# Samples' state increments as four 32-partition tiles, and other changes of order, in a one-core hybrid decoder layer

## The chip, the cores and the metric

The kernel runs on one core of a Trainium2 chip. Its time is device microseconds of one execution; the median of 3 runs of the kernel before is 1911.06 us (1909.26 to 1911.51). PE is the matrix engine (TensorE), DVE the vector engine, ACT the scalar engine, POOL GpSimd, SP the engine that issues the DMAs.

## What is computed

One layer is applied to a prompt (1 sequence of 1024 tokens) and to a group of samples (8 sequences of 8 new tokens, with caches and states). Both go through the same weights, so the kernel lays the 64 sample tokens behind the 1024 prompt tokens: 1088 columns. The layer projects to q, k, v, to a gate, to the state-space inputs z, x, B, C, dt and to two merge gates; it runs dilated window attention in three groups and a Mamba-2 scan (SSD), projects both branches, merges them and projects once more:

```python
# per state-space head group; b sequences, c chunks, l and s tokens, n = 128 states, p = 64
cb = jnp.einsum('bclgn,bcsgn->bcgls', cm, bm)
y_diag = jnp.einsum('bcgls,bgecls,bcsgep->bclgep', cb, decay, xdt)
decay_to_end = jnp.exp(da_cs[..., -1:] - da_cs)
states = jnp.einsum('bclgn,bgecl,bclgep->bcgepn', bm, decay_to_end, xdt)
def step(carry, inp):
    tot, st = inp
    return jnp.exp(tot)[..., None, None] * carry + st, carry
final, prev = lax.scan(step, init, ...)
y_off = jnp.einsum('bclgn,bcgepn,bgecl->bclgep', cm, prev, jnp.exp(da_cs))
...
merged = jax.nn.sigmoid(g_a) * a_out + jax.nn.sigmoid(g_b) * m_out
return x + gate[:, None, :] * (merged @ w_out)
```

For the samples a chunk is one sequence of 8 tokens. `states` of a sample is then a product over those 8 tokens only: its 128 states by the 128 channels of two heads. The sum of the decayed old state and this increment is an output for each sample and head.

## The kernel before

**Tiles.** Channels lie on the partitions, the 1088 tokens along the row, cut into chunks of 368, 368 and 352 columns for projections. A projection of 128 output channels takes 8 input tiles x 3 chunks x 3 matmuls (`mm3`, L195 to L200): weights and activations are split in a high and a low fp32r half, and high*high, low*high and high*low are summed in a PSUM bank named `pj`. The other matmuls have fp32 operands and go through `mm` (L206) or, as transposes, through `turn` (L210); both lines stand for many places, so the names of the tiles tell the places apart.

**Order.** On PE the order is the order of the Python calls, as long as `region` (L481 to L1105) is open. The projections run in a fixed list (`run`, L260). Between them a small planner, `Order` (L58), slips in the side work, which is written as generators: each `yield ns,` in such a generator asks that so many planned nanoseconds of projections pass before the next piece; `yield key, ns` counts them from the end of a named projection. The planner's nanoseconds are constants of the code. DVE, ACT, POOL and SP are ordered by a scheduler.

**Stages.** After norms and early projections (to about 65 us) comes attention with the projections of q, k, v (to 768 us), the state-space stage with the projections of B, C, x and z (to about 1545 us), the two branch projections and the output projection `fo` (to 1902.5 us).

**Attention** (`prompt_group`, L590). For each head pair and group, `scores(i)` makes scores s with two row tiles of 64 partitions (one per head) and the exponentials pr on DVE and ACT; `turned(i)` transposes pr through the bank pt to pT; `values(i)` makes o with column tiles of 64. The loop at its end calls `values(i - 2)`, `turned(i - 1)` and `scores(i)`.

**State space** (`side`, L924, and `x_tile`, L962). There are four groups. Each makes B and C (`conv_job`, L844), turns B's tokens onto the partitions (`to_tokens`, bank tt, result Bk), and makes C's products with B (bank cb). Then come four tiles of x, two heads each. A tile loads the decay table `csb` by DMA from `cs_d` (L965) and prepares it on DVE (L969, L972), ACT and DVE; turns its tokens (tt, result xdt); makes the prompt's chunk states stt (16 instructions) and scans them on DVE to sta; makes the samples' output yo from the old states sst (16 instructions on four column tiles of 32); then yo from sta, the transposes yoT, and the samples' increments sts; last, yd, the product with `csb`. After four tiles, the sum of squares `sq` (added up on POOL, L1098) goes through the ones-matmul ms (`sums`, L162) to the root-mean-square.

**Samples' increments before** (L1003 to L1012, L1063 to L1067). The 8 sequences share one contraction over 128 rows: 64 tokens' high part and 64 tokens' low part, `Bs`. So that a sequence only sees its own tokens, xd is rounded to a high part on ACT, the rest taken on DVE, and POOL multiplies both with a mask into two tiles `xdm` of 8 x 128 columns (8 POOL instructions per x-tile). Four fp32r matmuls of 512 columns follow right behind yoT, and two DVE adds.

**Output** (L1194 to L1212). For the sample tokens (t == 8) each quarter of 256 columns sums 24 matmuls with 64 stationary columns: high*high, low*high, high*low over 8 input tiles.

## Time and profile before

| | us |
|---|---|
| median of 3 runs | 1911.06 (1909.26 to 1911.51) |
| the profiled execution | 1912.37 |
| its span | 1910.6 |
| PE busy | 1871.7 (98%) |
| DVE busy | 1023.6 (54%) |
| ACT busy | 665.1 (35%) |
| POOL busy | 359.7 (19%) |

The trace comes from one execution. Its span is the time from the first to the last instruction that it shows; 1.8 us of the execution lie around it. Matmul durations in the trace overlap one another: two matmuls that start 0.16 us apart each show some 0.33 us. What a matmul takes on PE is therefore read from the starts, or from the chain of waits, whose pieces follow each other without overlap. An fp32 matmul shows as two instructions, an fp32r matmul and a transpose as one. The granted clock is 1.00 at 2.4 GHz and 0.50 at 1.2 GHz; a mean in between is a stretch that has some of both.

### The profile page before, as it was taken

To read this page: it belongs to the slowest core of one execution; us is meant where nothing else is said; L and a number is where in the kernel's file an instruction comes from. 1 tells how busy PE (TensorE), PEld (TensorE's weight loads), DVE (VectorE), ACT (ScalarE), POOL (GpSimd) and SP (SyncE) were. 2 spreads that over 40 slices of the span, in tenths; PEclk is the share of its full clock that TensorE was granted. 3 is DMA by queue.
4 is the path that set the end of the run, shared out by engine and by line. 5 is a ranking of instruction groups with operands and counts; after the bars stand their busy time and mean duration, and the time that the engine had idled before them with its cause. 6 is when DMAs were issued, how large, how long until landed. Compare 5 with 4: busy or idle time off the path is not lost.

```text
span 1910.6 us, 32219 instructions
## 1 busy us (share of the span) xinstructions
PE 1871.7 (98%) x13057; PEld 1747.7 (91%) x13057; DVE 1023.6 (54%) x1946; ACT 665.1 (35%) x1275; POOL 359.7 (19%) x576
## 2 busy tenths in 40 slices
PE   6999999999999999999999999999999999999998
PEld 4999989988998999999989998999898999999987
DVE  4633343325324322566675777577757666566654
ACT  4444233313423332424343435243434332131222
POOL 3100000000000000134513442444244300001300
PEclk8999999999999999999999999999999999999999
DMA  8422462273246227434443444444233364364322
GB/s 331 140 79 93 156 205 77 86 227 121 97 158 197 84 90 242 149 124 170 147 140 132 155 151 137 138 140 135 86 104 104 120 236 143 124 198 144 120 89 78
DMA packets 108949, 269.57 MB, mean 141 GB/s; under 512 B 41580, under 2 KB 50592, under 8 KB 105536
## 3 DMA queue, kind: packets, MB, share of 16 engines
q1 hardware_dynamic: 108800, 267.51, 42.3%
q8 instruction: 102, 1.67, 0.4%
q14 instruction: 47, 0.39, 0.1%
HBM read 224.93 MB, written 80.26 MB: 160 GB/s over the span
## 4 chain that ended last, share of the span: by engine, by line
PE 87%; DVE 5%; DMA 4%; ACT 2%; issue 1%; POOL 1%; SPq 0%; ACTq 0%; POOLq 0%; DVEq 0%
PE pj L198 22%; PE pj L199 21%; PE pj L200 21%; PE o L207 2%; PE pt L211 2%; PE s L207 2%; PE fo L1208 2%; PE fo L1206 2%; PE fo L1207 2%; PE yo L207 2%; DMA csb<-cs_d 2%; PE yd L207 2%; PE early L242 1%; PE stt L207 1%; PE tt L211 1%
## 5 line engine op out<-in xcount | busy, mean ns | idle before, releaser
L198 PE MATMUL pj<-h_hi,whi 128*128 128x368 f32 x2256 | 753.4, 334 | 0.0
L199 PE MATMUL pj<-h_hi,wlo 128*128 128x368 f32 x2256 | 738.4, 327 | 0.0
L200 PE MATMUL pj<-h_lo,whi 128*128 128x368 f32 x2256 | 738.4, 327 | 0.0
L198 PEld LDWEIGHTS pj<-h_hi,whi 128*128 128x128 f32 x2256 | 424.3, 188 | 25.5 <-issue 23.0
L199 PEld LDWEIGHTS pj<-h_hi,wlo 128*128 128x128 f32 x2256 | 424.6, 188 | 0.7
L200 PEld LDWEIGHTS pj<-h_lo,whi 128*128 128x128 f32 x2256 | 424.1, 188 | 0.0
L192 DVE TENSOR_TENSOR wlo<-wraw,whi 128x1024 fp32r<-128x1024 f32 (+1 forms) x136 | 151.0, 1110 | 204.9 <-ACT whi L191 203.0
L191 ACT ACTIVATE whi<-wraw 128x1024 fp32r<-128x1024 f32 (+1 forms) x136 | 126.5, 930 | 326.8 <-PE pj L200 262.5
L198 PE MATMUL pj<-yhi,whi 128*128 128x368 f32 (+1 forms) x480 | 157.7, 329 | 0.7 <-DVE acc L1170 0.7
L199 PE MATMUL pj<-yhi,wlo 128*128 128x368 f32 (+1 forms) x480 | 157.2, 327 | 0.0
L200 PE MATMUL pj<-ylo,whi 128*128 128x368 f32 (+1 forms) x480 | 156.9, 327 | 0.0
L620 ACT ACTIVATE pr<-pr,st 128x128 f32<-128x128 f32 (+1 forms) x192 | 83.9, 438 | 69.0 <-DVE st L617 68.9
L639 DVE COPY pT<-pt 128x512 f32<-128x512 f32 x40 | 27.6, 690 | 137.6 <-PE pt L211 64.0
L198 PEld LDWEIGHTS pj<-yhi,whi 128*128 128x128 f32 x480 | 90.1, 188 | 3.7 <-issue 2.1
L199 PEld LDWEIGHTS pj<-yhi,wlo 128*128 128x128 f32 x480 | 90.1, 188 | 1.5 <-issue 0.8
L200 PEld LDWEIGHTS pj<-ylo,whi 128*128 128x128 f32 x480 | 90.1, 188 | 0.0
L874 DVE SCALAR_TENSOR_TENSOR xc<-raw,cw,xc 128x1112 f32<-128x1112 f32 x60 | 82.5, 1375 | 12.3 <-ACT xc L872 11.5
L559 POOL COPY ks<-k 128x64 f32<-128x64 f32 x12 | 3.7, 306 | 379.2 <-DVE k L500 379.2
L1175 POOL TENSOR_TENSOR acc<-acc,ta 128x368 f32<-128x368 f32 (+1 forms) x24 | 24.2, 1009 | 249.2 <-DVE ta L1174 249.2
L969 DVE TENSOR_TENSOR csb<-tok,csb 128x2048 f32<-128x2048 f32 x16 | 39.6, 2477 | 55.3 <-DMA csb<-cs_d 55.3
L1002 POOL TENSOR_TENSOR xde<-xdt,tok 128x256 f32<-128x256 f32 x64 | 45.3, 734 | 115.9 <-DVE xdt L995 115.9
L500 DVE COPY k<-pj 128x368 f32<-128x368 f32 (+2 forms) x44 | 24.0, 581 | 75.0 <-PE pj L200 72.5
(269 smaller groups left out, 2596.6 us busy)
## 6 DMA issues: line engine op xcount, KB each, us to landing
wraw<-in_w_in SPq DMA_DIRECT2D x96, 512.0 KB, 4.4
csb<-cs_d SPq DMA_DIRECT2D x16, 1088.0 KB
kt<-in_kc SPq DMA_DIRECT2D x32, 448.0 KB, 4.6
out_kc<-in_kc SPq DMA_DIRECT2D x32, 448.0 KB, 5.0
out_vc<-in_vc SPq DMA_DIRECT2D x28, 512.0 KB, 4.7
vt<-in_vc SPq DMA_DIRECT2D x28, 512.0 KB, 5.5
sg_d<-sg SPq DMA_DIRECT2D x16, 544.0 KB, 2.7
ecs<-cs_d SPq DMA_DIRECT2D x32, 272.0 KB, 3.9
```

What stands on the lines that cost most here:

```text
L191: S.activation(hi, raw, AF.Copy)
L192: V.tensor_sub(lo, raw, hi.bitcast(F32))
L198: PE.matmul(ps, whi[:, k, :], xhi[k], start=first and k == 0, stop=False)
L199: PE.matmul(ps, wlo[:, k, :], xhi[k], start=False, stop=False)
L200: PE.matmul(ps, whi[:, k, :], xlo[k], start=False, stop=last and k == n - 1)
L207: PE.matmul(out, w, x, **kw)
L211: PE.transpose(out, x, eye)
L620: S.activation(pr[:, h, c0:c0 + m], pr[:, h, c0:c0 + m], AF.Exp, scale=-1.0, bias=st[:, 0, h, u:u + 1], accum_out=st[:, 1, h, u:u + 1])
L874: V.scalar_tensor_tensor(c, raw[:, t:t + CONV], cw[:, j, t:t + 1], c, op0=OP.mult, op1=OP.add)
L969: V.tensor_tensor(csb[:, :, :T].rearrange("p h (c l) -> p h c l", l=CH), tok[:, :8, 32 + h0:34 + h0].rearrange("p c h -> p h c")[:, :, :, ...
L1002: G.tensor_tensor(xde[:, c:c + 2].rearrange("p c (h d) -> p c h d", h=2), xdt[:, c:c + 2, :].rearrange("p c (h d) -> p c h d", h=2), tok[: ...
L1206: PE.matmul(ps, hi, whi[:, k, cs], start=k == 0, stop=False)
```

## The change

1. The 64 sample tokens stand in four groups of 32 partitions, 16 used in each (two sequences), instead of twice 64 partitions (`rows` and `natural`). Masks of two columns (`rmask`) replace those of eight. The samples' products cb and yd run over 128 rows, with zeros in between.
2. The increments are eight fp32 matmuls of 32 rows by 128 columns at four row positions into four banks. xd is made by two masked DVE multiplications; the rounding, the subtraction, the wide masks and `Bs` go. The block has a `yield` of its own behind yoT.
3. In attention `scores(i)` stands ahead of `turned(i - 1)`, and its exponentials behind that (`exponents`).
4. Two due times: 4000 to 7000 ahead of ms, 6000 to 4500 ahead of yd.
5. The samples' output projection has high and low halves side by side as 128 stationary columns (`smp`): 8 matmuls with the weights' high part per quarter, of which the low half is copied out, multiplied and added apart; then 8 with the weights' low part and 64 columns.

```diff
@@ prompt_group
                 if i > 1:
                     values(i - 2)
+
+                if i < nb:
+                    scores(i)
                 if 0 < i <= nb:
                     turned(i - 1)
                 if i < nb:
-                    scores(i)
+                    exponents(i)
@@ side
-                Bs = b1.tile([128, 128], F32R, tag="Bs", name="Bs")
-                S.activation(Bs, Bk[:, 8, :], AF.Copy)
-                V.tensor_sub(Bs[TS:], Bk[TS:, 8, :], Bs[TS:].bitcast(F32))
...
-                mm(ps[:TS, :TS], BS[:, :TS], CS[:, :TS], 224.0, start=True, stop=True)
-                V.tensor_tensor(CB[:TS, T:], ps[:TS, :TS], P("causal_s")[:TS], op=OP.mult)
+                mm(ps[:, :TS], BS, CS[:, :TS], 224.0, start=True, stop=True)
+                V.tensor_tensor(CB[:, T:], ps[:, :TS], P("causal_s"), op=OP.mult)
...
-                yield 4000.0,
+                yield 7000.0,
                 ps = bankB("ms")
@@ x_tile
-            V.tensor_tensor(xd.rearrange("p (h d) -> p h d", h=2), xdt[:, 8, :].rearrange("p (h d) -> p h d", h=2),
-                            tok[:, 8, 64 + h0:66 + h0, None].to_broadcast([128, 2, 64]), op=OP.mult)
-            S.activation(xdh, xd, AF.Copy)
-            V.tensor_sub(xd, xd, xdh.bitcast(F32))
-            for o, i in zip(xdm, (xdh.bitcast(F32), xd)):
-                for b in range(0, NB, 2):
-                    G.tensor_tensor(o[:, b:b + 2], i[:, None, :].to_broadcast([128, 2, 128]),
-                                    P("bmask")[:, b:b + 2, None].to_broadcast([128, 2, 128]), op=OP.mult)
+            for r in range(2):
+                V.scalar_tensor_tensor(xd[:, r].rearrange("p (h d) -> p h d", h=2),
+                                       xdt[:, 8, :].rearrange("p (h d) -> p h d", h=2), P("rmask")[:, r:r + 1],
+                                       tok[:, 8, 64 + h0:66 + h0, None].to_broadcast([128, 2, 64]), op0=OP.mult, op1=OP.mult)
...
-            for q in range(2):
-                ps = bankA("sts").rearrange("p (c n) -> p c n", c=4)
-                for i in range(2):
-                    mm(ps, Bs, xdm[i][:, 4 * q:4 * q + 4, :], 235.0, start=i == 0, stop=i == 1)
-                V.tensor_add(sst[:, 4 * q:4 * q + 4, :], sst[:, 4 * q:4 * q + 4, :], ps)
+            yield 2500.0,
+
+            ps = [bankA("sts"), bankB("sts"), bankA("sts"), bankB("sts")]
+            for r in range(2):
+                for j in range(4):
+                    rs = slice(32 * j, 32 * j + 32)
+                    mm(ps[j][:, r * 128:(r + 1) * 128], Bk[rs, 8, :], xd[rs, r, :], 65.0, start=True, stop=True,
+                       tile_position=(32 * j, 0))
+            for j in range(4):
+                V.tensor_add(sst[:, 2 * j:2 * j + 2, :], sst[:, 2 * j:2 * j + 2, :],
+                             ps[j][:, :256].rearrange("p (r n) -> p r n", r=2))
...
-            yield 6000.0,
+            yield 4500.0,
             for q in range(3):
                 ps = bankA("yd")
@@ output projection, t == 8
+                for k in range(KO):
+                    PE.matmul(ps[:, :w], smp[:, k, :], whi[:, k, cs], start=k == 0, stop=k == KO - 1)
+                low = f2.tile([TS, w], F32, tag="low", name="low")
+                S.activation(low, ps[TS:, :w], AF.Copy)
+                V.tensor_tensor(low, low, gbs[:, cs], op=OP.mult)
+                V.tensor_tensor(x[:n, cs], x[:n, cs], low, op=OP.add)
+                for k in range(KO):
+                    PE.matmul(ps[:n, :w], smp[:, k, :TS], wlo[:, k, cs], start=False, stop=k == KO - 1,
+                              skip_group_check=True)
```

Three places in the order. The first is PE in the state-space stage, at the end of the first x-tile's yo: `yo<-CT,sta` is the prompt's product with the states, `pj` a projection. Before:

```order
L200 MATMUL pj<-h_lo_102,whi 128x368
L207 MATMUL yo<-CT,sta 128x128 x7
L211 MATMUL yoT<-pack,ys 128x128 x2
L207 MATMUL sts<-xdm_7764,Bs 128x512
L207 MATMUL sts<-xdm_7765,Bs 128x512
```

After, the same place, and then the place of sts:

```order
L200 MATMUL pj<-h_lo_102,whi 128x368
L207 MATMUL yo<-CT,sta 128x128 x7
L211 MATMUL yoT<-pack,ys 128x128 x2
L198 MATMUL pj<-h_hi_95,whi 128x368
L199 MATMUL pj<-h_hi_95,wlo 128x368
```

```order
L199 MATMUL pj<-h_hi_92,wlo 128x352
L200 MATMUL pj<-h_lo_100,whi 128x352
L207 MATMUL sts<-xd,Bk 128x128 x8
L198 MATMUL pj<-h_hi_93,whi 128x352
L199 MATMUL pj<-h_hi_93,wlo 128x352
```

The sts matmuls (four before, in two pairs) stood directly behind yoT; now eight stand 18 projection matmuls further on, and 30 more projections lie between them and yd (39 between sts and yd before).

The second place is PE at the end of a group of four x-tiles, where ms sums the squares. Before:

```order
L199 MATMUL pj<-h_hi_91,wlo 128x352
L200 MATMUL pj<-h_lo_99,whi 128x352
L165 MATMUL ms<-sq,onesc 32x272 x4
L198 MATMUL pj<-h_hi_92,whi 128x352
L199 MATMUL pj<-h_hi_92,wlo 128x352
```

After:

```order
L200 MATMUL pj<-h_lo_100,whi 128x368
L165 MATMUL ms<-sq,onesc 32x272 x4
L211 MATMUL tt<-pack,xc 128x128 x8
L211 MATMUL tt<-pack,xcs 128x128
L198 MATMUL pj<-h_hi_93,whi 128x368
```

ms stood 27 projections behind the last yd, and the transposes tt of the next group's B another 27 behind ms; now 45 projections separate yd from ms, and tt follows ms directly. In the same way tt of the third tile of each group stands 30 projections behind yd, where 51 were. The last group's ms also has 45 ahead, and 87 behind it until the projections of y begin (27 and 141 before).

The third place is ACT at the start of the second group, around C's convolution `CT` and the decay table `csb`. L975 and L976 are csb's two passes, L872 is CT's first pass, L191 rounds a weight tile, and L155 is the root for ms. Before:

```order
L975 ACTIVATE csb<-csb 128x1088 x2
L155 ACT_TABLE_LOAD
L155 ACTIVATE ms<-ms 128x272
L976 ACT_TABLE_LOAD
L976 ACTIVATE csb<-csb 128x1088 x2
L191 ACTIVATE whi<-wraw 128x1024
L857 ACTIVATE raw<-pj 128x288
L859 ACTIVATE raw<-pj 128x8x8
L929 ACTIVATE Bk<-tt 128x512 x2
L929 ACTIVATE Bk<-tt 128x128
L872 ACTIVATE CT<-raw,cb,cw 128x1112
```

After (the same lines are L986, L987, L885, L155, L945 there):

```order
L986 ACTIVATE csb<-csb 128x1088 x2
L885 ACTIVATE CT<-raw,cb,cw 128x1112
L945 ACTIVATE Bk<-tt 128x512
L987 ACTIVATE csb<-csb 128x1088
L155 ACT_TABLE_LOAD
L155 ACTIVATE ms<-ms 128x272
```

CT's first pass moved ahead of the root, of csb's second pass and of Bk's copies; the weight's rounding no longer stands between.

In attention the order is that of the diff: 16 blocks of o, pt, s become o, s, pt, and 12 blocks of pt, s become s, pt. In the output projection the matmuls of the samples now stand as 24 with the high part (three quarters), 8 with the low part (the first quarter), 8 high (the last), 24 low.

## Rows read from the trace of the kernel before

**Rows 1.** The page: engines' busy time, and the chain's shares by engine

```profile
PE 1871.7 (98%) x13057; PEld 1747.7 (91%) x13057; DVE 1023.6 (54%) x1946; ACT 665.1 (35%) x1275; POOL 359.7 (19%) x576
...
PE 87%; DVE 5%; DMA 4%; ACT 2%; issue 1%; POOL 1%; SPq 0%; ACTq 0%; POOLq 0%; DVEq 0%
```

**Rows 2.** The chain of waits in attention: start us, us until the next piece, what

```profile
104.21 0.37 PE pj L198
...
360.21 0.87 PE pt L211 x8
361.08 1.09 PE s L207 x16
...
371.40 1.02 PE pt L211 x8
372.42 0.17 PE pj L198
```

**Rows 3.** PE's waits in attention: us in total, times, longest

```profile
PE pt L211 <- ACT pr L620: 2.7, 3, 1.0
```

**Rows 4.** The chain within one x-tile of the state-space stage

```profile
1053.78 1.78 PE stt L207 x16
1055.56 0.57 PE yo L207 x16
1056.13 0.36 PE pj L198
...
1066.43 0.22 PE yoT L211 x2
1066.65 0.93 PE sts L207 x4
1067.58 0.16 PE pj L198
```

**Rows 5.** POOL by line and form: busy us, mean ns | idle before

```profile
L1011 POOL TENSOR_TENSOR xdm<-xdh,pack 128x256 fp32r<-128x256 f32 x64 | 46.0, 747 | 7.3 <-ACT xdh L1007 7.3
```

**Rows 6.** PE's waits from 768 to 1560 us

```profile
PE yo L207 <- DVE sta L1028: 3.1, 3, 1.2
PE cb L207 <- DVE CT L881: 2.5, 1, 2.5
PE ms L165 <- POOL raw L850: 2.1, 1, 2.1
PE ms L165 <- POOL sq L1098: 2.1, 1, 2.1
```

**Rows 7.** The chain from 960 to 1560 us, longest pieces in order of time

```profile
967.09 7.67 DMA csb<-cs_d
...
995.54 3.83 PE cb L207 x18
...
1345.70 4.23 POOL sq L1098 x3
1349.99 0.84 PE ms L165 x2
...
1370.60 2.04 PE cb L207 x18
...
1443.04 1.71 PE sts L207 x4
```

**Rows 8.** PE's timeline at the last ms: start us, us, instruction

```profile
1530.24 2.15 PE L165 MATMUL ms<-sq,onesc 128*32 128x272 f32 x8
```

**Rows 9.** A window after 1350 us: busy us per engine, granted clock (PEclk), DMA share, GB/s

```profile
1350.00:1354.00 4.00, 4.00 (x14) 3.37 (x15) 0.52 (x2) 3.87 (x4) 0.15 (x1) 0.57 0.60 142
```

**Rows 10.** Timelines of DVE and PE where the projections of y begin

```profile
1554.53 2.56 DVE L1114 TENSOR_TENSOR ylo<-yx,yhi 128x1088 fp32r<-128x1088 f32 x2
...
1556.31 0.43 PE L198 MATMUL pj<-yhi,whi 128*128 128x368 f32 x1
```

**Rows 11.** The chain in the samples' output projection

```profile
1902.31 0.12 PE fo L1208
```

More of the change, by code (lines that the diff above doesn't have):

```diff
@@ L372, in trunk, with rows, natural @@
     tok = const.tile([128, 9, 96], F32, name="tok")
+    def rows(ap, first=0):
+        return ap.rearrange("p (j r s) -> p j r s", j=4, s=NS)[:, :, first:first + 2]
+    def natural(ap):
+        return ap.rearrange("p (j r s) -> p j r s", r=2, s=NS)
     def dt_tables(ap_):
@@ L424, in dt_tables @@
         S.activation(st[64:96], u, AF.Exp)
+        sts = ap_.tile([96, 128], F32, tag="dtst", name="dtst", bufs=1)
+        G.memset(sts, 0.0)
+        V.tensor_copy(rows(sts), natural(st[:, T:]))
         et = ap_.tile([32, 16], F32, tag="dtet", name="dtet", bufs=1)
@@ L612, in scores, with exponents @@
                            start=True, stop=True)
+            def exponents(i):
+                us = range(i * per, i * per + per)
+                ps = sps.pop(i)
                 pr = prs[i] = ap_.tile([128, 2, 512], F32, tag="pr", name="pr", bufs=1)
@@ L842, in trunk, with conv_job @@
         tiles = {}
-        def conv_job(name, j, marks, late, dst):
+        def conv_job(name, j, marks, late, dst, by_row=True):
             def make():
@@ L876, in after @@
                 S.activation(th, c, AF.Tanh)
-                a = bass.AP(tensor=th.tensor, offset=th[:, T + 3:].offset, ap=[th.ap[0], [NS + 3, NB], [1, NS]])
-                b = bass.AP(tensor=c.tensor, offset=c[:, T + 3:].offset, ap=[c.ap[0], [NS + 3, NB], [1, NS]])
-                V.scalar_tensor_tensor(cs[:, :TS].rearrange("p (b s) -> p b s", b=NB), a, 1.0, b, op0=OP.add, op1=OP.mult)
-                G.tensor_copy(cs[:, TS:], cs[:, :TS])
+                a, b = (bass.AP(tensor=x.tensor, offset=x[:, T + 3:].offset,
+                                ap=[x.ap[0], [2 * (NS + 3), 4], [NS + 3, 2], [1, NS]]) for x in (th, c))
+                V.scalar_tensor_tensor(rows(cs) if by_row else natural(cs[:, :TS]), a, 1.0, b, op0=OP.add, op1=OP.mult)
+                if by_row:
+                    G.tensor_copy(rows(cs, 2), rows(cs))
+                else:
+                    G.tensor_copy(cs[:, TS:], cs[:, :TS])
                 V.scalar_tensor_tensor(c[:, :T], th[:, :T], 1.0, c[:, :T], op0=OP.add, op1=OP.mult)
@@ L989, in x_tile @@
             xde = b1.tile([128, 8, 128], F32, tag="xde", name="xde")
-            xd = b1.tile([128, 128], F32, tag="xd", name="xd")
-            xdh = b1.tile([128, 128], F32R, tag="xdh", name="xdh")
-            xdm = [b1.tile([128, NB, 128], F32R, tag=f"xdm{i}", name=f"xdm{i}") for i in range(2)]
+            xd = b1.tile([128, 2, 128], F32, tag="xd", name="xd")
             def fin(c0, n, ps):
@@ L1082, in x_tile @@
                         mm(ps[h * 64:h * 64 + 64, (c % 4) * 128:(c % 4) * 128 + n],
-                           xdt[:n, c, h * 64:h * 64 + 64], mt[h][:n, c * 128:c * 128 + n], 115.0, start=True, stop=True)
+                           xdt[:, c, h * 64:h * 64 + 64], mt[h][:, c * 128:c * 128 + n], 115.0, start=True, stop=True)
                 V.tensor_add(u[:, 512 * q:512 * q + w], u[:, 512 * q:512 * q + w], ps[:, :w])
@@ L1180, in trunk @@
                     mlo.append(b)
+                    if m == 0:
+                        smp = acp.tile([128, KO, 2 * TS], F32R, tag="smp", name="smp")
+                    S.activation(smp[:, m, :TS], a[:, T:].bitcast(F32), AF.Copy)
+                    S.activation(smp[:, m, TS:], b[:, T:].bitcast(F32), AF.Copy)
     fp = ctx.enter_context(pool("fin", 1))
@@ L1200, in trunk @@
         for i in range(m):
-            ps = bankA("fo")[:n, :w]
+            ps = bankA("fo")
             cs = slice(i * w, (i + 1) * w)
-            for k in range(KO):
+            if t == 8:
+                for k in range(KO):
[7 more added lines that the diff above has]
+                              skip_group_check=True)
+            ps = ps[:n, :w]
+            for k in range(KO if t < 8 else 0):
                 hi = mhi[k][:, t * 128:t * 128 + n]
@@ L1269, in _constants @@
     s = np.arange(TS)
+    row = s // 16 * 32 + s % 16
     cs = np.zeros((128, TS), f)
-    cs[:TS] = (s[None, :] >= s[:, None]) & (s[None, :] // NS == s[:, None] // NS)
+    cs[row] = (s[None, :] >= s[:, None]) & (s[None, :] // NS == s[:, None] // NS)
     out["causal_s"] = cs
-    bm = np.zeros((128, NB), f)
-    bm[s, s // NS] = bm[TS + s, s // NS] = 1
-    out["bmask"] = bm
+    rm = np.zeros((128, 2), f)
+    rm[row, s // NS % 2] = 1
+    out["rmask"] = rm
     out["ident"] = np.eye(128, dtype=f)
```

28 lines of the change are left out of this document (12 added, 16 removed).

## The prediction

> **What bounds the kernel now.** I read the page's first and fourth part first: PE is busy 98% of the span, and the chain of work that ended last is PE for 87% of it [rows 1]. So the kernel costs what PE issues, plus the places where PE waits. Then I read the chain piece by piece. PE pieces there run from start to start, so a projection matmul (pj) of 0.16 to 0.17 us is its pitch, and the table of forms, whose 330 ns are overlapping durations, is no use for sums. The chain shows what a change of matmul kind costs: a pj behind scores (s) takes 0.37 instead of 0.17, a pj behind transposes (pt) takes no more than usual, and eight pt take 0.87 behind pj and 1.02 behind o [rows 2]. Last I read PE's waits: 2.7 us for exponents in attention [rows 3], and in the state-space stage 3.1, 2.5, 2.1 and 2.1 us [rows 6]. DVE (54% busy), ACT (35%) and POOL (19%) matter where one of those waits ends on them.
>
> The sum is made against the profiled execution: 1912.4 us, of which 1910.6 is the span. The median of the runs shown is 1911.06, 1.3 less, and the forecast goes down by that.
>
> **Attention: scores ahead of transposes.** By the order, 28 blocks change from "pt, s, projections" to "s, pt, projections"; 16 of them have o in front, 12 begin right behind projections. The arithmetic is the same, so only the changes of kind count. With o in front, pt stood behind another side kind before and does so now (1.02 each), s likewise (1.09 behind pt [rows 2]; behind o I assume the same), and the 0.20 us behind s (0.37 less 0.17) goes, since pt leaves none: 16 x 0.20 = 3.2 us. Without o, pt loses its cheap place behind pj (0.87 to 1.02), so 0.20 - 0.15 = 0.05 is left: 12 x 0.05 = 0.6. Besides, pt(i-1) now stands one s block (about 1.1 us) later behind the exponents it waits for. Three waits sum to 2.7 us with the longest 1.0 [rows 3], so each could be covered; but the exponents of the next block move behind, and DVE's bias ops sit between, so I take 2.0. What is late next would be pr of the following block, which has the 33 projections or more of a gap (5.5 us) ahead of it, as before. **Attention gives 5.8 us** (3.2 to 6.5).
>
> **Sample increments (sts).** Removed per x-tile: four wide matmuls, 0.93 us between yoT and a pj that pays no extra [rows 4], so 0.93 x 16. Added: a block of its own, eight fp32 matmuls of 32 rows x 128 x 128, which by the form of the other fp32 matmuls are 16 instructions. No row shows four 32-row tiles. Bounds: (a) four at a time, as in the 16 yo instructions on four 32-column tiles, 0.57, plus 0.20 for the pj behind (0.36 against 0.16) = 0.77 [rows 4]; (b) two at a time, as the 16 s instructions on two 64-row tiles, 1.09 + 0.20 = 1.29 [rows 2]; (c) one after another, as 16 stt instructions, 1.78 + 0.20 = 1.98 [rows 4]. Row (a) has as many tiles but a stationary of 32 columns, row (b) has the 128 columns. I take the middle of these two, 1.03, which is 0.10 x 16 = **1.6 us lost** (2.6 gained by a, 5.8 lost by b, 16.8 lost by c).
>
> The Trainium skill, "TensorE: Matmul & The Clock Gate", Part 3 (Measured speedup vs the span model), gives 3.07 times for four tiles with K=32; as an estimate from that page the block would be 1.78/3.07 + 0.20 = 0.78, and the forecast 4 us lower. "TensorEngine Tiling (Array Packing)", Key Properties, says on the other hand that a change of tiling mode drains the engine; the 0.20 us behind s agrees, and the change makes 16 more such places.
>
> The other engines: POOL loses its masks (46.0 us for the high halves alone [rows 5], as many ops again for the low), ACT the rounding copy, DVE a subtraction; DVE gains a second masked multiply and has four smaller adds. None of it is on the chain by itself. The block needs four PSUM banks at once; their last readers are a whole stage earlier in the ring, and 18 projections (about 3 us) lie between yoT and sts, so I price that at nothing. If the cover were gone, PE would stand behind DVE's add and every projection behind it.
>
> **Sums of squares (ms).** In the second and third group the last add of sq on POOL is late: from the first ms to the last pair 4.23 us pass [rows 7], where eight undisturbed ms take 2.15 [rows 8], of which three quarters are 1.6. So 2.6 us are lost, twice: 5.2. After the later of the two the granted clock is 0.57 over 4 us [rows 9], partly the 1.2 GHz level, which loses 0.43 x 4 = 1.7 more. The change lets 45 projections instead of 27 run between yd and ms: 18 x 0.165 = 3.0 us, just over the 2.6. Then sq is ready in time, and the pause with its clock goes too: 6.9 us. As ms now stands in one block with tt, three times an exit of 0.20 is saved: 0.6. **7.5 us** (1 to 8).
>
> **C's scores (cb) and yo.** In the second group cb waits 2.5 us for CT [rows 6] and then runs 3.83 instead of 2.04, at half clock [rows 7]: 4.3 us. Ahead of it lie a csb load of 7.67 us and what DVE and ACT do with csb. By the order ACT now takes CT's first pass ahead of csb's exponentials, of ms's root and of the weights' rounding, which stood between; I count 3.9. The yo waits for sta are 3.1 us in three [rows 6], behind which sts ran 1.71 instead of 0.93 [rows 7]: 3.9, and some projections at the lower clock, about 0.6. Their cause, csb landing late, stays, and only DVE's and POOL's smaller load speaks for a gain: I take 1.9 of 4.5. **5.8 us** (1 to 8.5).
>
> **Samples' output projection.** 96 matmuls of 256 columns become 64 with the same columns, the pitch is 0.12 [rows 11]: 32 x 0.12 = 3.8. Three of the four second passes have another quarter's first pass ahead of them, so ACT's copy is hidden there; for the first a wait of a few tenths is possible. **3.6 us** (2.5 to 3.8). The low half's two DVE ops per quarter lie beside the second pass.
>
> **New waits.** (1) The third tile of each group has tt 30 projections after yd instead of 51; its xdt needs DVE behind csb's long ops. (2) y's projections begin 132 instead of 168 matmuls after the last yd, 6 us less cover; the last ylo pair starts at 1554.53 for 2.6 us, the first y matmul at 1556.31 [rows 10], so the cover was already thin, though the loads for it are issued earlier now. (3) cb of the other groups. I give 1.0, 1.0 and 0.5: **2.5 us lost** (0 to 9).
>
> Sum: 5.8 - 1.6 + 7.5 + 5.8 + 3.6 - 2.5 = 18.6. Profiled: 1912.4 - 18.6 = 1893.8; median: **1892.5**.
>
> **Rivals.**
> - *The waits only move.* PE's waits in the state-space stage begin at csb's load, issued when yd frees its buffer (967.09, 7.67 us [rows 7]). The change does not shorten that, and takes away time between yd and later steps. Then most of the 6.9 + 5.8 us comes back at tt, cb, sta or the start of y: 1899 to 1905, centre 1902. For it: the DMA in the chain. Against it: POOL and ACT were the last steps at ms and cb, and both get shorter queues. Chance 0.20.
> - *Row tiles run two at a time* (bound b): 4.2 us more, 1896.7, inside the forecast's own range. *One after another* (bound c): 15.2 more, 1907.7, within 0.2% of before. Against it stands the s block, whose 64-row tiles take 1.09 us for 16 where stt needs 1.78. Chance of c: 0.06.
> - *Slower: each change of row tile costs what leaving a row-tiled block costs.* At the sts block, eight matmuls of two instructions at 0.111 (1.78/16) with 0.20 each: 3.4 us a tile instead of 1.03, 38 us in all, so 1930. It decides from 1.03 + 18.6/16 = 2.2 us a block on. Against it: s pays no such thing between its two tiles. Chance 0.05.
> - *More than forecast*: bound a, no new waits, all of yo: 4.2 + 2.5 + 2.6 less, about 1883. Chance 0.08.
>
> **How the numbers follow.** The forecast with its bounds (1886 to 1898) has 0.60, waits that only move 0.20, more 0.08, serial tiles 0.06, slower 0.05 or a little more for what I do not see. A measurement of this kernel tells 0.2%, 3.8 us, from no change, so faster means below 1907.2: 0.60 + 0.20 + 0.08 less a little = 0.87; same 0.07; slower 0.06. The range 1882 to 1905 leaves out the serial and the slower case and the edges of the others, under 0.2 together.
>
> **What would show it.** In the chain after: sts as a block of 0.77 to 1.29 (right), near 2 or 3.4 (rivals); pj behind pt at 0.17 and no 0.37 behind s in the changed blocks; no ms piece above 2.3 us; a single cb length of about 2.0; 64 fo matmuls in under 8 us. PE's waits in the state-space stage together under 4 us instead of 10. New waits at tt, cb, sta or at y's first matmuls with a sum above 6 us would make me wrong to the high side.

## The result, and the profile after

The changed kernel takes **1891.39 us** (median of 4 executions, 1889.56 to 1895.35), the kernel before, timed beside it, 1910.51 (4 executions, 1909.26 to 1911.51). The ratio is 0.9903, 95% interval 0.9887 to 0.9919: faster by 1.0%, clear of the noise, and within 1.1 us of the forecast. The profiled execution took 1892.67 us, its span is 1890.6, against 1893.8 forecast for it. That the sum came so close is in part luck: its terms were off in both directions, by up to 3.3 us, and most of these errors cancelled.

The page of the changed kernel, parts 1 and 4 (as [rows 1]):

```profile
PE 1853.4 (98%) x13217; PEld 1736.5 (92%) x13217; DVE 1020.6 (54%) x1983; ACT 663.4 (35%) x1275; POOL 271.5 (14%) x445
...
PE 90%; DMA 5%; DVE 2%; issue 1%; ACT 1%; SPq 0%; POOL 0%; ACTq 0%; DVEq 0%
```

PE is still the bound: 18.3 us less busy of the 20.0 us that the span lost. The span in stages, in us, read from the starts of the named matmuls in both traces:

| stage | before | after | difference |
|---|---|---|---|
| attention: first s to last so (samples' attention included) | 671.6 | 664.8 | -6.8 |
| from there to the first tt | 39.2 | 40.2 | +1.0 |
| state space: first tt to last yd, and on to the first y matmul | 728.5 and 30.7 | 720.7 and 22.8 | -15.7 |
| y's projections, to the first fo | 245.3 | 250.0 | +4.7 |
| fo, first to last | 100.9 | 97.0 | -3.9 |
| from there to the end | 8.1 | 9.3 | +1.2 |

The third line is two stretches, because 36 projections (6 us) moved from the second of them into the first; only their sum can be compared. Y's projections lose part of what the state-space stage gains (the waits for the gate below), so these two lines are read together: 11.0 us gained. The first s itself stands 0.4 us earlier.

The chain of waits in attention after (as [rows 2]; start us, us until the next piece, what):

```profile
100.26 0.86 PE o L207 x12
101.12 1.06 PE s L207 x8
102.18 1.02 PE pt L211 x8
103.20 0.18 PE pj L198
```

Scores stand ahead of transposes, and the projection behind the transposes takes 0.18, where the one behind scores took 0.37. The wait for exponents of [rows 3] is gone from PE's waits altogether.

PE's waits from 768 to 1560 us after (as [rows 6]; us in total, times, longest):

```profile
PE tt L211 <- DVE ms L170: 5.9, 3, 2.6
PE gate L471 <- DMA wg<-in_w_gate: 3.1, 2, 1.7
PE pj L198 <- ACT yhi L1125: 1.2, 1, 1.2
PE tt L211 <- DVE xc L897: 0.7, 1, 0.7
PE yo L207 <- DVE sta L1034: 0.4, 1, 0.4
PE pj L198 <- ACT raw L870: 0.4, 1, 0.4
```

The waits at ms and cb are gone and the one at yo is nearly gone, as forecast. But the sum is 11.7 us where it was about 10 (7.4 of the 11.7 without the gate and y's first matmul): there are two large new waits, at tt for ms and at the gate, for causes that the prediction didn't name. The first is seen in PE's timeline at the end of the second group (start us, us, instruction; in brackets the idle time before it and what ended it), the second fence is DVE's timeline of the same stretch:

```profile
969.24 0.67 PE L165 MATMUL ms<-sq,onesc 128*32 128x272 f32 x8
969.84 1.09 PE L211 MATMUL tt<-pack,xc 128*128 128x128 f32 x8
972.77 0.33 PE L211 MATMUL tt<-pack,xcs 128*128 128x128 f32 x1 [1.84 <-DVE ms L170]
```

```profile
968.73 2.29 DVE L980 TENSOR_TENSOR csb<-tok,csb 128x2048 f32<-128x2048 f32 x1 [4.08 <-DMA csb<-cs_d]
...
971.14 1.23 DVE L192 TENSOR_TENSOR wlo<-wraw,whi 128x1024 fp32r<-128x1024 f32 x1
972.29 0.43 DVE L170 TENSOR_SCALAR ms<-ms 128x272 f32<-128x272 f32 x1
```

A ring is a set of PSUM banks that are handed out in turn. Ring B has three in this stage; tt needs all three, and ms has just taken one. So the ninth transpose needs ms's bank again, which DVE frees at L170; DVE first does csb and then the low half of a weight tile (wlo). Every projection behind that transpose waits too, and after PE's idle 1.84 us the granted clock falls, as a window of the changed kernel shows (us, busy us of PE, PEld, DVE, ACT and POOL, granted clock, DMA share, GB/s):

```profile
974.00:978.00 4.00, 4.00 (x16) 4.00 (x15) 2.92 (x3) 3.97 (x6) 0.00 (x0) 0.57 0.61 245
```

### The profile page after: what moved, and what is told of

Its sections match the earlier page's. It is cut to its first block, busy times and chain, and to the rows that moved or that the text cites. A ratio compares the mean times of both kernels' runs of the same rounds, so it can differ in the third digit from the quotient of the medians.

```text
span 1890.6 us, 32497 instructions
## 1 busy us (share of the span) xinstructions
PE 1853.4 (98%) x13217; PEld 1736.5 (92%) x13217; DVE 1020.6 (54%) x1983; ACT 663.4 (35%) x1275; POOL 271.5 (14%) x445
## 4 chain that ended last, share of the span: by engine, by line
PE 90%; DMA 5%; DVE 2%; issue 1%; ACT 1%; SPq 0%; POOL 0%; ACTq 0%; DVEq 0%
PE pj L198 23%; PE pj L199 22%; PE pj L200 22%; PE s L207 2%; PE o L207 2%; DMA csb<-cs_d 2%; PE pt L211 2%; PE yd L207 2%; PE yo L207 2%; PE fo L1237 2%; PE fo L1238 2%; PE fo L1236 2%; PE stt L207 1%; PE early L242 1%; PE tt L211 1%
## 5 line engine op out<-in xcount | busy, mean ns | idle before, releaser
L191 ACT ACTIVATE whi<-wraw 128x1024 fp32r<-128x1024 f32 (+1 forms) x136 | 126.5, 930 | 336.8 <-PE pj L200 283.6
L506 DVE COPY k<-pj 128x368 f32<-128x368 f32 (+2 forms) x44 | 23.9, 579 | 73.9 <-PE pj L200 70.7
L1067 POOL TENSOR_TENSOR sst<-sst,eall 128x256 f32<-128x256 f32 x64 | 49.9, 810 | 69.9 <-PE yo L207 67.6
L1034 DVE SCALAR_TENSOR_TENSOR sta<-sta,eall,stt 128x64 f32<-128x64 f32 x224 | 45.1, 271 | 26.8 <-ACT sta L1030 26.8
```

The costliest lines, as they stand in the source:

```text
L191: S.activation(hi, raw, AF.Copy)
L1034: V.scalar_tensor_tensor(sta[:, i, hs], sta[:, i - 1, hs], eall[:, h0 + h, i:i + 1], ps[:, c, hs], op0=OP.mult, op1=OP.add)
L1067: G.tensor_tensor(part, part, etot[:, h0:h0 + 2, b:b + 2].rearrange("n h b -> n b h")[:, :, :, None] .to_broadcast([128, 2, 2, 64]), op=OP ...
```

## Experiments

Medians in us, with the kernel before as timed beside each run on the same chip. The kernel before itself came out between 1910.5 and 1913.7, so a difference of medians between rows with different values there carries up to 3 us of that; the ratios do not.

| run | median | before | ratio (95%) |
|---|---|---|---|
| e_attn | 1904.77 | 1913.04 | 0.9951 (0.9931 to 0.9971) |
| e_major | 1891.16 | 1913.04 | 0.9890 (0.9871 to 0.9908) |
| e_ms4000 | 1903.64 | 1913.04 | 0.9954 (0.9936 to 0.9971) |
| e_msbank | 1884.86 | 1913.04 | 0.9856 (0.9839 to 0.9872) |
| e_b7000 | 1910.36 | 1910.92 | 0.9993 (0.9980 to 1.0005) |
| e_sts | 1920.64 | 1910.92 | 1.0047 (1.0032 to 1.0062) |
| e_oldfo | 1894.30 | 1910.92 | 0.9911 (0.9896 to 0.9926) |
| e_best | 1893.38 | 1910.92 | 0.9903 (0.9888 to 0.9918) |
| e_ctpool | 1889.59 | 1913.74 | 0.9868 (0.9845 to 0.9890) |
| e_once | 1904.80 | 1913.74 | 0.9948 (0.9928 to 0.9967) |
| e_best2 | 1889.02 | 1913.74 | 0.9865 (0.9845 to 0.9885) |
| e_final | 1884.87 | 1912.77 | 0.9859 (0.9842 to 0.9877) |

**Attention alone** (e_attn), put into the kernel before:

```diff
                 if i > 1:
                     values(i - 2)
+                if i < nb:
+                    scores(i)
                 if 0 < i <= nb:
                     turned(i - 1)
                 if i < nb:
-                    scores(i)
+                    exponents(i)
```

> The kernel before with the attention part of the change alone (scores ahead of transposes, exponentials behind). Theory, the prediction's term: leaving the row-tiled block costs 0.20 us and goes in 28 blocks (3.8 us), and the waits of pt for the exponentials (2.7 us) go, so 5.8 to 7 us less than before (about 1904 us), from the first s to the last so some 665 us instead of 671.6. Rival: in the changed kernel the attention stage is shorter for other reasons (other loads, other buffers), and this edit alone gives the 3.8 us of the block changes at most, with PE's waits for pr still there.

The attention stage fell from 671.6 to 666.7 us, and of PE's waits for exponents none is left. By the ratio the gain is 5.5 to 13.2 us; 5.8 lies at its lower end. Counted around the blocks themselves, the 16 with o cost 44.6 instead of 47.7 us and the 12 without o 24.7 instead of 27.5, of which 2.7 is the wait: 5.9 us, against 5.8 forecast. The changed kernel shows the same two sums, 44.6 and 24.7. The stage's own total varies by about 1 us between traces of one order (670.9 to 672.7 with the old, 664.5 to 666.7 with the new). The rest of the ratio's middle lies outside attention (cb's wait was 0.6 in this trace instead of 2.5) and is not explained by this edit.

**The four row tiles in another order of issue** (e_major, of the changed kernel):

```diff
-            for r in range(2):
-                for j in range(4):
+            for j in range(4):
+                for r in range(2):
```

> The changed kernel with the eight sts matmuls issued tile by tile (both matmuls of a row tile behind each other) instead of in two rounds over the four tiles. Theory: PE starts matmuls in the order of issue, so two on the same row tile stand one behind the other and only neighbours on different tiles overlap; a block then takes about 1.4 us instead of 0.66, 12 us in all, 1903. Rival: each row tile runs on its own, the order within the block does not matter, and block and time stay (0.66 us, 1891).

The chain at the same place, first of the changed kernel, then of e_major:

```profile
840.98 0.66 PE sts L207 x16
841.63 0.36 PE pj L198
```

```profile
839.75 0.68 PE sts L207 x16
840.42 0.36 PE pj L198
```

0.66 and 0.68 us for 16 instructions: the rival held, and my theory of 1.4 us failed. The tiles run side by side whichever is issued first, no cost shows between tiles, and there is one 0.20 for the projection behind. In e_major's trace the starts come in groups of four, 13 or 14 ns apart (6 or 7 in the changed kernel), with 0.11 to 0.21 us from the first of a group to the first of the next. The instructions that report a tile's end are all four in the last group; so each group holds one instruction of each tile, although both matmuls of a tile were issued behind each other. That settles what the prediction had as two rivals: the tiles don't run one after another, and a change of row tile costs nothing that these blocks show.

**The bank of ms** (e_msbank, one word):

```diff
-                ps = bankB("ms")
+                ps = bankA("ms")
```

> The changed kernel with the sums' bank ms taken from ring A instead of ring B, so that the transposes tt behind it need not wait until DVE has read ms. Theory: PE's three waits of tt for DVE's read of ms (5.9 us in all, the tt block costing 3.4 to 4.4 us instead of about 1.6) are a bank's release and nothing else; they go, and the time falls by about 6 us, to 1885. Rival: the wait only moves to the next step that needs csb's engines (cb for CT, stt for xde, sta), and the time stays within 2 us.

PE's timeline at the same place as above:

```profile
969.72 0.67 PE L165 MATMUL ms<-sq,onesc 128*32 128x272 f32 x8
970.31 1.09 PE L211 MATMUL tt<-pack,xc 128*128 128x128 f32 x8
971.24 0.27 PE L211 MATMUL tt<-pack,xcs 128*128 128x128 f32 x1
```

The wait is gone in all three groups, and the clock in the window of 974 to 978 us is 1.00 again:

```profile
974.00:978.00 4.00, 4.00 (x26) 4.00 (x25) 2.49 (x2) 3.98 (x5) 0.00 (x0) 1.00 0.77 262
```

1884.86 against 1891.39 is 6.5 us by the medians, 9 by the ratios; the first tt to the last yd takes 7.4 less. That is the 5.9 of the wait and a little of the clock. This shows the bank to be the cause, and the kernel beats both others.

**The due time ahead of ms** (e_ms4000, the changed kernel with the old value; e_b7000, the kernel before with the new one):

```diff
-                yield 7000.0,
+                yield 4000.0,
```

> The changed kernel with the due time ahead of ms back at 4000 instead of 7000, nothing else: ms again 27 projections behind yd, the transposes in a block of their own. Theory: ms is paced by POOL's four adds of sq, so each ms block takes 2.2 us or more (instead of 0.6) and up to 5 where csb's op holds the last add, but tt's 5.9 us of waits for the bank go; the two cancel within 3 us (1888 to 1895). Rival, by the prediction's count: the later ms is worth 7.5 us, so the time goes up to about 1899.

> The kernel before with 7000 instead of 4000 ahead of ms, nothing else. Theory: ms finds sq ready (0.7 instead of 2.2 to 5.2 us a block), but tt behind it waits for ms's bank (some 2 us in each of three groups), and by the order CT stays behind csb's second pass on ACT, so that cb waits as before or longer: within 4 us of before. Rival: the due time alone is what the changed kernel gains in the state-space stage: 8 us or more less, 1902.

In e_ms4000 the ms blocks were not late (2.05 us each, the last 2.45; tt waits for ms's bank 0.2 us in all), but the time went up by 12 us by the medians, 10 by the ratios. The two halves of the theory did not cancel, and the rival's 1899 was nearer, for another cause: the loss is at another step, cb, whose four blocks cost 23.3 us instead of 7.7, waits and lower clock together. PE's longest waits from 768 us on in e_ms4000:

```profile
PE cb L207 <- DVE CT L897: 10.9, 3, 3.7
```

The chain of e_ms4000 in the second group shows why (start us, us, what):

```profile
974.41 0.30 ACT raw L870
974.84 1.28 ACT L987
976.13 2.11 ACT csb L987 x2
978.25 1.14 ACT Bk L945 x3
979.39 1.22 ACT CT L885
```

ACT starts CT at 979.39, behind csb's exponentials. With 7000, ACT's timeline of the changed kernel has C's evacuation `raw` at 968.81 instead of 974.41, and CT at 973.27:

```profile
968.81 0.39 ACT L870 ACTIVATE raw<-pj 128x288 f32<-128x288 f32 x1
971.26 2.11 ACT L986 ACTIVATE csb<-csb 128x1088 f32<-128x1088 f32 x2 [1.94 <-DVE csb L983]
973.27 1.30 ACT L885 ACTIVATE CT<-raw,cb,cw 128x1112 f32<-128x1112 f32 x1
```

PE ends C's projections at about 968 us in both traces; what differs is when ACT, which works in its written order, gets to them. So in the changed kernel the due time's value lies in C's projections, which stand ahead of ms and let ACT have CT 6 us earlier; not in the rest it gives POOL. In the kernel before the same value gained nothing clear of the noise: e_b7000 shows cb's wait at 9.4 us in three groups, and yo's still at 3.0. There the due time alone does not bring CT ahead. The wait of tt that I expected there is absent (tt does not stand behind ms in that kernel), and ms still waits twice, 0.9 us each.

Why the kernel before pays cb's wait in one group and these variants in three can be read from the starts in the traces. The table is for the second to fourth group, in us. The ms block is the one ahead of the group, from the projection before it to the one behind, less a pitch. "CT ready" (the end of DVE's last pass over it) and "cb starts" count from the last yd of the group before:

| kernel | cost of the ms block | CT ready | cb starts | PE waited for CT |
|---|---|---|---|---|
| before | 3.0, 5.0, 5.2 | 28.7, 26.6, 26.6 | 28.7, 28.1, 29.7 | 2.5, 0, 0 |
| e_b7000 | 2.2, 0.7, 2.2 | 27.9, 28.6, 27.9 | 27.9, 28.7, 27.9 | 2.5, 4.4, 2.5 |
| e_ms4000 | 2.0, 2.0, 2.0 | 27.8, 28.5, 27.2 | 27.9, 28.5, 27.2 | 3.7, 3.7, 3.4 |
| e_ctpool (below) | 2.0, 2.0, 2.0 | 25.6, 25.1, 24.5 | 25.7, 25.1, 24.5 | 1.6, 1.3, 0.8 |
| changed | 3.7, 4.4, 3.4 (with tt) | 22.6, 23.3, 22.1 | 25.8, 26.5, 23.9 | 0, 0, 0 |

In the kernel before CT is late in all three groups. In two of them ms holds PE for 5 us first, and PE comes to cb when CT is there. Where that wait at ms is gone, PE waits at cb instead. Between these two steps the waits only move, until ACT takes CT earlier.

**CT's first pass on POOL** (e_ctpool, an edit of e_ms4000):

```diff
-                S.activation(c, raw[:, :CONV], AF.Identity, scale=cw[:, j, 0:1], bias=cb[:, j:j + 1])
+                if name[0] == "C":
+                    G.tensor_scalar(c, raw[:, :CONV], cw[:, j, 0:1], cb[:, j:j + 1], op0=OP.mult, op1=OP.add)
+                else:
+                    S.activation(c, raw[:, :CONV], AF.Identity, scale=cw[:, j, 0:1], bias=cb[:, j:j + 1])
```

> The changed kernel with the due time of 4000 ahead of ms (as the run with that edit alone, 1903.6, where cb waits 10.9 us for CT), and with CT's first pass on POOL instead of ACT. Theory: cb waits because ACT, which works in order, reaches CT's first pass only behind the root for ms, two table loads, a weight's rounding, csb's second pass and Bk's copies (979.3 in that run, 973.3 in the changed kernel); on POOL it can start when C's evacuation is done (974.8), some 2.5 us long, so about 2 to 3 us of each of the three waits goes: 1895 to 1898. Rival: CT is late because of DVE (csb's op, ms's reciprocal) or because its projection ends later; then the waits stay, 1903.

14 us faster than e_ms4000 by the medians (16 by the ratios), more than expected:

```profile
PE cb L207 <- DVE CT L900: 3.7, 3, 1.6
```

PE waits 3.7 us for CT at cb there, in three groups, instead of 10.9. That is the expected 2 to 3 us less in each; beyond it, cb itself hardly runs at the lower clock any more, and its four blocks cost 12.2 us instead of 23.3. Taking CT off ACT's queue takes away most of the wait, so it was ACT's order that held cb. In the second group POOL's pass ends at 979.84 where ACT's ended at 980.61, only 0.8 us earlier by the clock of the trace; but all steps of this trace stand later there (C's last evacuation at 976.76 instead of 974.31). Counted from that evacuation CT's first pass ends 3.2 us earlier, from the last yd CT is ready 2.2 to 3.4 us earlier, as the table above shows.

**The first part of the change alone** (e_sts, the kernel before with the new layout of sample tokens, the row tiles, no masks, and the due times around them; attention, ms, fo and the gate's buffer as before):

```diff
-                mm(ps[:TS, :TS], BS[:, :TS], CS[:, :TS], 224.0, start=True, stop=True)
+                mm(ps[:, :TS], BS, CS[:, :TS], 224.0, start=True, stop=True)
...
+            yield 2500.0,
+            ps = [bankA("sts"), bankB("sts"), bankA("sts"), bankB("sts")]
...
+            yield 4500.0,
```

> The change's first part alone: samples' tokens as rows, the sts matmuls on four row tiles, no masks, with their two due times (2500, 4500); attention, the due time ahead of ms (4000), the output projection and the gate's buffer as before. Theory: the sts blocks cost 0.75 us instead of 1.0 (4 us less in 16 tiles), but with ms at 27 projections ACT takes CT's first pass behind csb's exponentials and the root again, and cb waits for CT in three groups (10.9 us with the due time of 4000); so 1908 to 1913, no gain to speak of. Rival: the new increments bring most of the change by freeing POOL, ACT and DVE: about 1900.

Slower by 0.47%. PE's longest waits from 768 us on:

```profile
PE cb L207 <- DVE CT L890: 10.9, 3, 3.7
PE pj L198 <- DVE acc L1176: 4.2, 1, 4.2
```

yo's wait falls from 3.1 to 0.4, and ms has none left: the four ms blocks cost 8.6 us instead of 15.4. The lighter load of POOL, ACT and DVE is the likely cause; this run moves sts as well, so it isn't shown apart. But cb pays in three groups (22.5 us instead of 12.8), and y's part has a wait of 4.2 at its first accumulation. The direction was expected, the size was not. With e_b7000: neither the new increments nor the due time helps cb alone; in the changed kernel, which has both, cb doesn't wait.

**sts directly behind yoT, as it was** (e_once, of the changed kernel):

```diff
-            yield 2500.0,
             ps = [bankA("sts"), bankB("sts"), bankA("sts"), bankB("sts")]
...
-            yield 4500.0,
+            yield 7000.0,
```

> The changed kernel with sts directly behind yoT as it was before (no due time of its own; 7000 ahead of yd, so that all else keeps its place). Theory: sts's last two banks are still read by DVE (the second half of yo), which ends about 0.6 us after yoT, so PE waits in each of the 16 tiles: 8 to 12 us more than the changed kernel, 1900. Rival: the banks are free, and one change of kind less per tile gives 0.1 us in each: 1889.5.

The chain of e_once in the same x-tile:

```profile
836.55 1.58 PE yo L207 x14
838.15 0.70 DVE u L1056
838.89 0.71 PE sts L207 x10
839.60 0.37 PE pj L198
```

sts waits for a bank that DVE (u, from yo) has not yet read. The block of yo, yoT and sts costs 3.25 us, the projection behind it included, instead of 1.79 and 0.86: 0.6 us in each of 16 tiles, 9.6 in all, as the theory said. Here is the cover that the prediction priced at nothing, and its cost without it. The whole kernel loses 13 us by the medians, 9 by the ratios; part of that (2.9 us of waits at ms for POOL's sq, 1.7 at yo) came with the moved order, which also takes away the 5.9 of tt.

**The old output projection** (e_oldfo, of the changed kernel):

```diff
-            ps = bankA("fo")
+            ps = bankA("fo")[:n, :w]
...
-            for k in range(KO if t < 8 else 0):
+            for k in range(KO):
```

> The changed kernel with the samples' output projection as before (96 matmuls, no stationary of 128 columns, no low copy). Theory: PE takes 3.9 us more from the first to the last fo, the tail behind the last fo is 1.2 us shorter (8.1 instead of 9.3, since the three last quarters then do not come to DVE together), so 2.7 us more: 1894. Rival: the tail has another cause (the buffers or the last output), stays at 9.3, and the time goes up by 3.9.

fo takes 100.7 us, the tail 8.0: PE loses 3.7, the tail gains 1.3. By the medians 2.9 us are lost, by the ratios 1.5, and the two intervals overlap, so it is the two stages that show the theory right, not the whole time. The chain of the changed kernel at its end (as [rows 11]):

```profile
1874.11 2.87 PE fo L1224 x24
1876.98 0.92 PE fo L1230 x8
1877.90 0.95 PE fo L1224 x8
1878.85 2.75 PE fo L1230 x24
```

64 matmuls in 7.5 us at the old pitch. But three second passes end in PE's last 2.75 us, and in DVE's timeline their ops stand behind one another, with no idle time before 1884.9.

**Three attempts at a better version.** e_best: ms in ring A, the gate's weights in the ring `yx` and one round later, and fo's passes staggered, one quarter's first pass ahead of each second pass.

```diff
-        wg = wgp.tile([128, D], F32, tag="smp", name="wg")
+        wg = wgp.tile([128, D], F32, tag="yx", name="wg")
...
-                if gr == 1:
-                    ada_gate(yw, acp, m, pg)
+                if gr == 2:
+                    ada_gate(yw, yr, m, pg)
...
```

> The changed kernel with three edits: ms in a bank of ring A; the gate's weights loaded in the ring of y's tiles during the third round of y's projections instead of the second, in a buffer that no DMA of the state-space stage holds; the samples' output projection with its low passes one quarter behind its high passes. Theory: 6 us from the bank, 3 us and two changes of kind from the gate (PE waits 3.1 us for its weights), 0.5 to 1.2 from the tail: 1881. Rivals: the gate's weights take the place of y's tiles in their ring, and PE waits for ylo instead (no gain from the gate, 1885); the low passes now wait for ACT's copy, and what the tail gains PE loses.

The wait for the gate's weights is gone, but y's projections take 257.2 us where e_msbank has 249.4: waits for yhi and for sums stand there instead (3.1 and 1.6 us up to 1660 us), much as the first rival said, though at a higher price than its 1885: the ring now feeds two. The stagger brings the tail to 9.1 from 9.3, no more.

e_best2: wg in a buffer of its own instead.

```diff
-        wg = wgp.tile([128, D], F32, tag="smp", name="wg")
+        wg = pool_.tile([128, D], F32, tag="wg", name="wg", bufs=1)
...
-        gt = pool_.tile([128, 256], F32, tag="gt", name="gt", bufs=1)
+        gt = wgp.tile([128, 256], F32, tag="smp", name="gt")
...
```

> The changed kernel with ms in a bank of ring A (1884.9 by itself), the gate's weights back in a buffer of their own and its bias tile in the room of smp instead, and the low passes of the output projection one quarter behind the high ones. Theory: PE's waits for the gate's weights (2.5 us in that run) go, with the first two gates no longer held by the DMA that empties sg, and the tail gives 0.2: 1882. Rival: the gate's weights, loaded earlier, crowd y's first tiles out of the DMA queues, PE waits for yhi or ylo instead, and the time stays at 1885.

The gate waits 0.5 us, but the first y matmul waits 4.6 us for yhi: again the rival.

e_final: ms in ring A, 6000 ahead of it, CT's first pass on POOL, fo staggered.

```diff
...
-                yield 7000.0,
-                ps = bankB("ms")
+                yield 6000.0,
+                ps = bankA("ms")
...
```

> The changed kernel with four edits: ms in a bank of ring A, 6000 instead of 7000 ahead of ms (which by the order also leaves only one of the gate's products early in y's projections instead of two), CT's first pass on POOL, and the low passes of the output projection one quarter behind the high ones. Theory: 6.5 us from the bank as in that run (1884.9), about 1 us less waiting of cb, 2 us from one wait for the gate's weights less, 0.2 from the tail: 1881 to 1883. Rival: with ms 6 projections earlier, PE waits for POOL's adds again (POOL now also has CT's pass), and csb, y or the gate take back what the others give: 1885 or more.

No wait at cb or at the gate, 712.1 us from the first tt to the last yd (e_msbank 713.3), and still 1884.87: PE waits 2.7 us for ylo and 1.4 for yhi where y's projections begin (251.1 us for these, e_msbank 249.4). What is taken away earlier returns at the first y matmuls, whose inputs come from loads, ACT and DVE. e_msbank, a single word, is as fast.

## Why the prediction was right, term by term

Measured values compare the two traces. They are PE's time from the projection ahead of each block to the one behind it, less a projection's pitch, summed over the blocks; for attention and sts the extra of the projection behind is included.

| term | forecast | measured | from |
|---|---|---|---|
| attention | 5.8 | 5.9 | 47.7 to 44.6 with o, 27.5 to 24.7 without |
| sts | -1.6 | 1.1 | 16 x (0.93 - 0.86) |
| ms with tt | 7.5 | 5.9 | 18.2 before, 12.2 after |
| cb and yo | 5.8 | 9.1 | cb 12.8 to 7.7; yo's stalls 5.2 to 1.2 |
| fo | 3.6 | 2.7 | 3.9 on PE, 1.2 lost in the tail |
| new waits | -2.5 | -4.5 | gate 3.3, yhi 1.2 |
| sum | 18.6 | 20.2 | the spans: 20.0 |

The 0.2 that is left over hides smaller shifts which cancel, such as the 1.0 lost between attention and the first tt. The errors of the terms, +0.1, +2.7, -1.6, +3.3, -0.9 and -2.0, come to +1.6. The number is thus better than the account behind it: by the prediction's own signs sts, pj behind pt, ms, cb and fo are as they should be, but PE's waits in the state-space stage are 7.4 us and not under 4, and the new ones at tt for ms and at y's first matmul (5.9 and 1.2) pass the 6 us that should have meant a time above the forecast.

- **Attention: right, by its mechanism.** o 0.86, s 1.06, pt 1.02, pj 0.18 in the chain are the four pieces as forecast. The blocks with o gave 3.1 (3.2 forecast). Those without gave 2.8, of which 2.7 is the wait (0.6 and 2.0 forecast): there the change of kind was worth 0.2 only, and all three waits went. e_attn shows the same block costs by itself.
- **sts: the choice between the bounds was wrong.** The step that failed is taking the middle of (a) and (b): the block takes 0.66 + 0.20 = 0.86, near (a), which has as many tiles, and far from (b), which has as wide a stationary. Whether the 0.09 above (a) comes from the width isn't shown. The 0.20 behind the block stood as read from s. The estimate from the Trainium skill, "TensorE: Matmul & The Clock Gate", Part 3 (Measured speedup vs the span model), was nearer, 0.78; in its terms, 1.78/0.66 = 2.7 times instead of 3.07, which the page gives for 512 columns where these matmuls have 128.
- **ms: the mechanism was half of it, and the size came out near by errors that cancel.** First, the "undisturbed" 2.15 us was itself paced: POOL's four adds ran from 1528.75 for 2.94 us (timeline of the kernel before) beside the eight ms. With sq ready, eight ms take 0.59, so all four groups gain and not two. In the last group of the changed kernel the chain has these two pieces:

```profile
1519.46 0.59 PE ms L165 x8
1520.06 0.36 PE pj L198
```

  Second, the 0.6 for fewer exits assumed that tt can follow ms without a pause. It can't, for the bank: 5.9 us, and two low clocks behind it (0.57 over 4 us in the window above, 0.64 in the next group). Without that, as e_msbank shows (5.6 us for ms and tt), the term would have been 12.5. Third, the late adds themselves went without the later due time: e_sts and e_ms4000 keep 4000, and their four ms blocks cost 8.6 us instead of 15.4. In the kernel before POOL's four adds of the third group took 4.96 us instead of 2.94, the last one 2.80 instead of 0.76, while DVE's csb op of 2.50 us ran; in e_sts and e_ms4000 the adds begin 3.1 us behind the last yd instead of 4.2, and are done before that op starts (6.8 to 8.1 us behind the yd; 6.0 to 8.0 in the kernel before). Which part of the new increments moved the adds isn't shown. The Trainium skill, "SBUF — State Buffer", Who interferes with whom, says that a DVE instruction with two SBUF inputs contends with a GpSimd instruction that reads SBUF; the adds of 4.96 and 2.94 us agree.
- **cb and yo: right in cause, too small.** ACT's earlier CT does what was said, and e_ctpool shows ACT's order to be the cause. All four cb blocks now take the same (1.95 in the chain). What I left out is that these waits would have grown to three groups without the new due time (e_ms4000), so in the changed kernel the due time is worth 10 to 12 us. At yo I gave 1.9 of 4.5; it gave 4.0. e_sts, with the new increments alone, has it already (the waits 3.1 to 0.4), but doesn't part the lighter DVE and POOL from the new place of sts.
- **fo: PE as worked out; the tail was put at nothing.** I asked whether a quarter's second pass would wait for ACT, and put DVE's two ops per quarter beside the second pass. When three quarters end together, DVE's ops stand behind PE's last matmul: 1.2 us.
- **New waits: the size low, the largest place missed.** None of the three named is large (tt for xc 0.7, where it was 0.4; cb none; y's start 1.2). The gate's weights are new. The list of the change doesn't name their move: `wg` was a buffer of its own in the pool of y's weights, and is now taken under the tag `smp` from a pool that opens only when the state-space stage has ended. In the changed kernel's chain the load of wg begins only when the write of sg has ended (start us, us),

```profile
1535.03 3.97 DMA sg_d<-sg
1539.02 4.50 DMA wg<-in_w_gate
1543.65 0.67 PE gate L471 x8
1544.34 5.93 DMA wg<-in_w_gate
```

  most likely because wg's buffer shares its room with what that write reads. e_best2, with a buffer of its own again, loads the first wg ahead of that write and has 0.5 us of waits left there.
- **The rivals.** "The waits only move" was the nearest: the sum of waits didn't fall, and between ms and cb it is just what happens in e_sts, e_ms4000 and e_b7000. It failed for the changed kernel since CT moved ahead on ACT, since the waits at ms were never the whole cost of ms, and since most of the lower clock at cb and behind yo went with the old waits. Serial tiles and a price for each change of tile are excluded by the changed kernel's block of 0.86 us, and e_major shows the same in another order.

## What to carry to other kernels

A due time in a written order moves every in-order engine behind it: ask which engine gets its next input earlier, not only which one gets a rest; here it was worth 10 to 12 us at a step that the edit doesn't mention, and nothing without the other edits. When one wait goes, look for the next step whose input is no earlier than before: PE will stand there instead. Where two blocks are put together, follow their banks round the ring to the last reader, and ask what stands ahead of that reader on its engine. Before a block is taken as the undisturbed price of its instructions, look for the engine that feeds it.

## What was unexpected of the hardware

- Sixteen fp32 instructions on four row tiles of 32 partitions (128 columns each) took 0.66 us in one order of issue and 0.68 in the other, and in both the starts come in fours, one of each tile; nothing in the traces marks the change from tile to tile. Only the projection behind them takes 0.36 instead of 0.16.
- Eight ms matmuls of 272 columns took 0.59 us with their input ready, against 2.15 where POOL was still adding.
- The same first pass of a convolution over 128 x 1112 took ACT 1.30 us and POOL 2.06 on average. The mean hides two cases: 1.28 us once, with DVE idle, and 2.32 to 2.33 three times, while DVE ran `wlo<-wraw,whi`, an op of two inputs in SBUF. POOL's line of e_ctpool (line, operation, tiles, count, busy us and mean ns, idle before):

```profile
L886 POOL TENSOR_SCALAR CT<-raw,cw,cb 128x1112 f32<-128x1112 f32 x4 | 8.3, 2064 | 0.0
```
